# Three token parts for all projection blocks, with the last part beside HGRN in an order written by hand

## The chip, the cores and the metric

The kernel runs on one core of one Trainium2 chip. The metric is the device time of one execution in microseconds (us). The core's engines are named as in the profile: PE (TensorE matmul), PEld (its weight load), DVE (VectorE), ACT (ScalarE), POOL (GpSimd) and SP (SyncE, which here only issues DMAs).

## The reference

One layer of a hybrid mixer over 2048 latent tokens and 256 context tokens of width 1024:

```python
p_lat = (_layer_norm(h_x) * (1.0 + sc_l[:, None]) + sh_l[:, None]) @ w_in[l]
p_ctx = (_layer_norm(h_ctx) * (1.0 + sc_c) + sh_c) @ w_in[l]
pv_l, u_l, fh_l, g_l = _split_proj(p_lat)
...
y_rc, y_rl = _rwkv_branch(u_c, u_l, ...)      # two directions, 6 heads of 64, a state per head
o_hc, o_hl = _hgrn_branch(fh_c, fh_l, ...)    # two directions, 6 heads of 64, chunkwise
pool_l = _pool_branch(pv_l, True, ...)        # centred means over windows of 2, 4, 8, 16
mix_l = jnp.concatenate([pool_l, y_rl, o_hl], axis=-1) * jax.nn.silu(g_l)
new_x = _layer_norm(ALPHA * h_x + gt_l[:, None] * (mix_l @ w_out[l])) * ln_g[l] + ln_b[l]
```

Both scans read the context first and go on over the latent tokens from the context's final state; only the latent output is returned.

## The kernel before

The input projection has 33 blocks of 128 output columns. A projection is made in two fp32r halves: the operands are split into a high part and a rest (`split`: ACT writes the high part, DVE or POOL the difference), and 24 matmuls (high by high, low by high, high by low, over eight slices of the 1024 inputs) sum into one PSUM tile.

The work stands in four stages.

1. *Input stage* (0 to about 500 us): norms, modulation, and the 11 RWKV blocks, group by group of 256 tokens. The modulated input is written to DRAM (`s_x`).
2. *RWKV* (about 500 to 1400): 36 chunks of 64 tokens for both directions. `start` makes the pair products of a chunk (L722, masked on DVE in L724), `gather` and `solve` invert the triangles of four chunks at a time on DVE (L779, L782), `merge` puts the halves together (L831, L841), `late` transposes keys (L744), and `step` carries the state (L858 to L899). The loop runs from n = -7 (`LEAD` chunks ahead) to 35.
3. *HGRN* (about 1400 to 1912): nine windows of 256 tokens for both directions, the first being the context. `hlevels` loads a window, prepares gates and scores and runs six levels; `hsteps` transposes keys, reads out and carries the state chunk by chunk.
4. *Output stage* (1912 to 2152): head norms, gates, the output projection, the last norm.

The other 22 blocks (q, z, i of HGRN, the pooled inputs, the gates) are made beside stages 2 and 3 by the generator `filler(parts, blocks)`. A part is a set of token pieces of up to 512 tokens, 768 in all. For each part `filler` loads the eight slices of the input from `s_x` and splits them into the tiles `fxh` and `fxl`, of which there is one set; then for each block it loads and splits the weights (one block ahead) and projects each piece. It yields after every six matmuls: such a stretch is called a step here, and four steps are a piece. Each piece ends in a sink: to DRAM as it is, to DRAM with tokens on partitions (`to_tokens`, with PE transposes), or through the pooling (`pooled`, scans and differences on DVE).

Before, there were two fillers. The first made 18 blocks (q, z, i, six gates) for three parts beside RWKV, the second made the pooled blocks and the last two gates for three parts of its own beside HGRN. `Beside` runs the steps that have fallen due when RWKV's loop calls it, at four places a chunk; a `BORDER` yield at a part's end makes it pause. In RWKV the order of PE is the order in which the code is written (`manual_schedule`); in HGRN a plan of numbers (`H_LEV`, `H_STP`, `H_FIL`, `H_OW`) gave the order to the scheduler, which placed the instructions of PE, too, by its own estimates. The other engines are ordered by the scheduler throughout. All loads and most stores are issued on SP's queue.

Of the kernel before, what the change touches and what calls it, by code (L numbers as in the profile page):

```python
# [20 lines left out]
P = 128  # L21
D = 1024
KB = 8
# [20 lines left out]
HOLD = 1  # L44

NG_R = 6

# [92 lines left out]
def hybrid_block(ctx: ExitStack, tc: tile.TileContext, x, ctxt, mod_w, w_in, w_up, a_up, pool_w,  # L140
# [388 lines left out]
    def filler(parts, blocks):  # L529

        for part in parts:
            n_all = sum(n for _, n in part)
            xh, xl = [], []
            for k in range(KB):
                xh.append(big.tile([P, FTOK], F32R, name=f"fxh{k}"))
                xl.append(big.tile([P, FTOK], F32R, name=f"fxl{k}"))
                xs = fp.tile([P, FTOK], F32, name="fxs", bufs=2)
                o = 0
                for t0, n in part:
                    QX.dma_start(out=xs[:, o:o + n], in_=s_x[:, k, t0:t0 + n])  # L540
                    o += n
                split(xs[:, 0:n_all], xh[k][:, 0:n_all], xl[k][:, 0:n_all], V)
# [9 lines left out]
            yield BORDER  # L552
# [82 lines left out]
    class Beside:  # L635


        def __init__(self, gen):
            self.gen, self.due, self.hold = gen, 0.0, 0

        def __call__(self, k):
            self.due += k
            if self.hold:
                self.hold -= 1
                return
            while self.due >= 1:
                self.due -= 1
                if next(self.gen, 0) == BORDER:
                    self.hold = HOLD
                    return  # L650
# [17 lines left out]
    with ExitStack() as ph:  # L668
# [239 lines left out]
        def once(f, n):  # L908
# [3 lines left out]
        parts = [[(T, TCTX), (0, 512)], [(512, 512), (1024, 256)], [(1280, 256), (1536, 512)]]  # L912
# [8 lines left out]
        fill1 = filler(parts, blocks)  # L921
        fill = chain(fill1, filler(parts2, blocks2))
# [13 lines left out]
        def beside(n, k):  # L936
            if n >= R_FIL[0]:
                pace(k * R_FIL[1])


        go("sc", 0, start)
        with tc.manual_schedule(engines={mybir.EngineType.PE}):
            for n in range(-LEAD, NCH):
# [33 lines left out]
            run(fill1)  # L977
# [3 lines left out]
    with ExitStack() as ph:  # L981
# [18 lines left out]
        V.tensor_tensor(out=hsl, in0=blk1[:, 0:P:64].unsqueeze(1).broadcast_to([P, 2 * NPR, 2]),  # L1000
                        in1=lb1.unsqueeze(2).broadcast_to([P, 2 * NPR, 2]), op=ALU.mult)
        hdone = [0, 0]

        def hlevels(d, n, w):
# [19 lines left out]
            if lat:  # L1024
                q = fq.tile([P, NPR, HWIN], F32, name=f"q{d}")
                SP.dma_start(out=q, in_=s_q[:, :, tsl].rearrange("b p t -> p b t"))
                qp = wk.tile([P, NPR, HWIN], F32, name=f"qp{d}")
# [23 lines left out]
            if lat:  # L1051
                pd = psl.tile([P, 2, NPR, nm], F32, name="pl")
                for m in range(nm):
                    for p in range(NPR):
                        PE.matmul(pd[:, :, p, m], q[:, p, P * m:P * m + P], hsl[:, 3 * d + p, :], start=True, stop=True)
                V.tensor_tensor(out=sc.rearrange("q h p m t -> q (h p m) t"),
                                in0=cst[:, C_DIAG].unsqueeze(1).broadcast_to([P, 2 * NPR * nm, CH]),
                                in1=pd.rearrange("q h p m -> q (h p m)").unsqueeze(2).broadcast_to(
                                    [P, 2 * NPR * nm, CH]), op=ALU.mult)
# [17 lines left out]
        def hsteps(d, n, w):  # L1077
            lat, tw, t0, ks, it, tot = w["lat"], w["tw"], w["t0"], w["ks"], w["it"], w["tot"]
            kt = stp.tile([P, NPR, nm, P], F32, name=f"kt{d}", bufs=1)
            for p in range(NPR):  # L1080
                pt = pst.tile([P, 512], F32, name="pa")[:, 0:HWIN].rearrange("q (m c) -> q m c", c=P)
                for m in range(tw // P):
# [240 lines left out]
```

## Time and profile before

| | us |
|---|---|
| median of 3 runs (lowest, highest) | 2149.41 (2149.09, 2152.09) |
| profiled execution | 2153.85 |
| its span | 2151.8 |
| PE busy | 1877.4 (87%) |
| DVE busy | 1470.2 (68%) |
| ACT busy | 954.1 (44%) |
| POOL busy | 808.4 (38%) |

Busy times are sums over the whole span and say nothing of the stages apart. PE's clock has two levels, 2.4 and 1.2 GHz; a granted clock of 0.9 is a mean over stretches at 1.0 and at 0.5. Most fp32 matmuls stand in the trace as two records, the fp32r matmuls of the projections as one.

### The profile page before, as it was taken

To read this page: it belongs to the slowest core of one execution; us is meant where nothing else is said; L and a number is where in the kernel's file an instruction comes from. 1 tells how busy PE (TensorE), PEld (TensorE's weight loads), DVE (VectorE), ACT (ScalarE), POOL (GpSimd) and SP (SyncE) were. 2 spreads that over 40 slices of the span, in tenths; PEclk is the share of its full clock that TensorE was granted. 3 is DMA by queue.
4 is the path that set the end of the run, shared out by engine and by line. 5 is a ranking of instruction groups with operands and counts; after the bars stand their busy time and mean duration, and the time that the engine had idled before them with its cause. 6 is when DMAs were issued, how large, how long until landed. Compare 5 with 4: busy or idle time off the path is not lost. (4 is left out here: it accounts for less than half of the span.)

```text
span 2151.8 us, 46723 instructions
## 1 busy us (share of the span) xinstructions
PE 1877.4 (87%) x18306; PEld 1593.8 (74%) x18306; DVE 1470.2 (68%) x3045; ACT 954.1 (44%) x1809; POOL 808.4 (38%) x729
## 2 busy tenths in 40 slices
PE   4788899994989979999979999968989998878996
PEld 1677788893777768877868788757877776657896
DVE  2788899886546646475473762189788788879862
ACT  3876786663123333333333233455444645322321
POOL 0144355545211322322323323454334435624653
PEclk7899999996999989999979999968888997589998
DMA  6544444328655565655666444442322323545531
GB/s 247 195 136 144 142 131 126 106 74 252 187 147 150 171 184 164 182 143 164 174 180 192 139 129 136 152 132 82 109 81 70 124 80 115 176 150 187 194 128 59
DMA packets 290915, 313.68 MB, mean 146 GB/s; under 512 B 85572, under 2 KB 246468, under 8 KB 289672
## 3 DMA queue, kind: packets, MB, share of 16 engines
q1 hardware_dynamic: 280680, 280.29, 43.3%
q10 hardware_dynamic: 4896, 17.83, 2.5%
q0 software_dynamic: 5120, 12.59, 1.8%
q8 instruction: 144, 2.36, 0.5%
q14 instruction: 75, 0.61, 0.1%
HBM read 213.88 MB, written 96.74 MB: 144 GB/s over the span
## 5 line engine op out<-in xcount | busy, mean ns | idle before, releaser
L220 POOL TENSOR_TENSOR fwl<-fwf,fwh 128x1024 fp32r<-128x1024 f32 x66 | 158.7, 2405 | 422.3 <-ACT fwh L219 369.3
L565 PE MATMUL fps<-fxh,fwh 128*128 128x512 f32 (+1 forms) x952 | 230.7, 375 | 31.0 <-ACT fxh L219 28.4
L565 PE MATMUL fps<-fxl,fwh 128*128 128x512 f32 (+1 forms) x952 | 217.2, 362 | 0.0
L565 PE MATMUL fps<-fxh,fwl 128*128 128x512 f32 (+1 forms) x952 | 211.6, 357 | 0.0
L565 PEld LDWEIGHTS fps<-fxh,fwh 128*128 128x128 f32 x952 | 160.4, 201 | 63.4 <-ACT fxh L219 34.7
L565 PEld LDWEIGHTS fps<-fxl,fwh 128*128 128x128 f32 x952 | 160.2, 199 | 24.1 <-issue 1.0
L565 PEld LDWEIGHTS fps<-fxh,fwl 128*128 128x128 f32 x952 | 158.7, 196 | 23.8
L779 DVE TENSOR_TENSOR tm<-m,o 96x31 f32<-96x31 f32 (+15 forms) x279 | 117.4, 421 | 60.3 <-DMA m<-sd 52.2
L904 POOL TENSOR_TENSOR ys<-ys,pp 64x384 f32<-64x384 f32 x64 | 76.6, 1196 | 198.7 <-ACT ys L901 191.6
L336 PE MATMUL ps<-xh,wh 128*128 128x258 f32 x768 | 125.4, 304 | 17.5 <-ACT wh L219 11.9
L1116 DVE SCALAR_TENSOR_TENSOR sbd<-sbd,tot,ps 64x64 f32<-64x64 f32 x432 | 120.5, 279 | 25.7 <-PE ps L1111 16.7
L1044 PE MATMUL pl<-qb,ks 128*64 128x64 f32 x2304 | 108.4, 252 | 30.3 <-DVE sc L1046 22.9
L1039 ACT COPY qb<-qp 64x384 f32<-64x384 f32 x192 | 99.6, 519 | 77.7 <-DVE qp L1069 33.8
L724 DVE TENSOR_TENSOR at<-pa,cst 128x384 f32<-128x384 f32 x144 | 74.1, 548 | 81.9 <-PE pa L722 81.8
L336 PEld LDWEIGHTS ps<-xh,wh 128*128 128x128 f32 x768 | 106.0, 198 | 30.6 <-ACT wh L219 13.3
L1044 PEld LDWEIGHTS pl<-qb,ks 128*64 128x64 f32 x2304 | 94.1, 161 | 45.5 <-issue 29.3
L782 DVE TENSOR_TENSOR o<-o,tm 96x31 f32<-96x31 f32 (+15 forms) x279 | 115.8, 415 | 8.3
L336 PE MATMUL ps<-xh,wl 128*128 128x258 f32 x768 | 118.6, 294 | 0.0
L1069 POOL TENSOR_TENSOR ks<-ks,tot 128x384 f32<-128x384 f32 x90 | 90.5, 1014 | 74.6 <-PE pl L1044 72.7
L336 PE MATMUL ps<-xl,wh 128*128 128x258 f32 x768 | 116.0, 289 | 0.0
L336 PEld LDWEIGHTS ps<-xh,wl 128*128 128x128 f32 x768 | 104.6, 196 | 5.7 <-issue 5.2
L336 PEld LDWEIGHTS ps<-xl,wh 128*128 128x128 f32 x768 | 102.3, 192 | 4.9 <-issue 4.6
(230 smaller groups left out, 4449.0 us busy)
## 6 DMA issues: line engine op xcount, KB each, us to landing
fwf<-in_w_in_dram SPq DMA_DIRECT2D x66, 512.0 KB, 4.2
xt<-in_x_dram ACTq DMA_DIRECT2D x32, 512.0 KB, 4.9
s_kr<-kr SPq DMA_DIRECT2D x54, 256.0 KB, 2.3
s_bk<-bk SPq DMA_DIRECT2D x54, 256.0 KB, 2.5
bks<-s_bk SPq DMA_DIRECT2D x72, 192.0 KB, 3.2
krs<-s_kr SPq DMA_DIRECT2D x72, 192.0 KB, 3.5
bk<-s_bk SPq DMA_DIRECT2D x72, 192.0 KB, 3.0
kr<-s_kr SPq DMA_DIRECT2D x72, 192.0 KB, 3.1
```

Of the source, the lines that this page charges most:

```text
L220: eng.tensor_tensor(out=wl, in0=wf, in1=wh.bitcast(F32), op=ALU.subtract)
L336: PE.matmul(ps[:, 0:TG + 2], a[:, k, :], b[:, k, :], start=(i == 0), stop=(i == 23))
L565: PE.matmul(ps[:, 0:n], a[:, k, :], b[k][:, o:o + n], start=(i == 0), stop=(i == 23))
L724: V.tensor_tensor(out=at[:, h], in0=pa[h], in1=cst[:, C_MASK[d]].unsqueeze(1).broadcast_to([P, NPR, P]), op=ALU.mult)
L779: V.tensor_tensor(out=tv, in0=m[:, j:j + 1, j + 1:32].broadcast_to([nrow, na, nb]), in1=o[:, 0:na, j:j + 1].broadcast_to([nrow, na, nb]), ...
L782: V.tensor_tensor(out=o[:, 0:na, j + 1:32], in0=o[:, 0:na, j + 1:32], in1=tv, op=ALU.subtract)
L904: G.tensor_tensor(out=ys[vr], in0=ys[vr], in1=pp[d][vr], op=ALU.add)
L1039: S.copy(out=qb[hh, :, :, h, :].rearrange("q p c (i b) -> q (p c) i b", b=b), in_=src[hh].rearrange("q p (c i j b) -> q (p c) i j b", c=nc ...
L1044: PE.matmul(pl[64 * (c % 2):64 * (c % 2) + 64, :, p, c // 2, :], ks[:, p, CH * c:CH * c + CH], qb[:, p, c, :, :], start=True, stop=True)
L1069: eng.tensor_tensor(out=v_, in0=v_, in1=tv[:, :, :, 1 - par:2 - par].broadcast_to([P, NPR, nb, b]), op=ALU.mult)
L1116: V.scalar_tensor_tensor(out=sn[hh, p, hh], in0=so_[hh, p, hh], scalar=tot[hh, p, c:c + 1], in1=ps[hh, p, :], op0=ALU.mult, op1=ALU.add)
```

## The change

There is one filler: all 22 blocks for each of three parts (context with tokens 0 to 511; 1280 to 2047; 512 to 1279). Its steps are spread over RWKV and HGRN. Inputs are loaded two slices ahead, across parts too, and the split comes in four pieces of two slices, each ended by a `BORDER`; the pause after a border is gone. RWKV begins with the first part's splits and 20 steps, and then takes 7.6 steps a chunk where it took 9.4. In HGRN the order of PE is written by hand: a window has 14 slots, each with a state step or key transposes of the last window (k, s), a level of this window (l) and `H_FIL` filler steps; the output weights come in the ninth window's slots. The diagonal scores of a window are made with the weights' and the data's roles exchanged, and key transposes are copied out of PSUM in two pieces in place of three.

```diff
-R_FIL = (-6, 9.4)
-H_LEV = (-0.3508, 0.112, 0.0116)
-H_STP = (-0.224, 0.296, 0.047)
-H_FIL = (-0.255, 10.317)
-H_OW = (6.2029, 10.25)
+R_FIL = (20, 7.6)
+H_FIL = (2.2, 1.9, 1.0)
...
-        for part in parts:
+        xs = [load(parts[0], k) for k in range(2)]
+        for pi, part in enumerate(parts):
...
-                split(xs[:, 0:n_all], xh[k][:, 0:n_all], xl[k][:, 0:n_all], V)
+                split(xs[k % 2][:, 0:n_all], xh[k][:, 0:n_all], xl[k][:, 0:n_all], V)
+                if k + 2 < KB:
+                    xs[k % 2] = load(part, k + 2)
+                elif pi + 1 < len(parts):
+                    xs[k % 2] = load(parts[pi + 1], k % 2)
+                if k % 2:
+                    yield BORDER
...
-        parts = [[(T, TCTX), (0, 512)], [(512, 512), (1024, 256)], [(1280, 256), (1536, 512)]]
+        parts = [[(T, TCTX), (0, 512)], [(1280, 256), (1536, 512)], [(512, 512), (1024, 256)]]
...
-                 [(B_G + b, to_dram(s_g[b], AF.Silu)) for b in range(NG_R)]
-        parts2 = [[(0, 512), (512, 256)], [(768, 256), (1024, 512)], [(1536, 512)]]
-        blocks2 = [(B_POOL + b, pooled(b)) for b in range(2)] + \
-                  [(B_G + b, to_dram(s_g[b], AF.Silu)) for b in range(NG_R, 8)]
+                 [(B_POOL + b, pooled(b)) for b in range(2)] + \
+                 [(B_G + b, to_dram(s_g[b], AF.Silu)) for b in range(8)]
...
+            for _ in range(KB // 2):
+                pace(0)
+                next(fill)
+            run(fill, R_FIL[0])
             for n in range(-LEAD, NCH):
...
-            run(fill1)
...
-        hsl = rc.tile([P, 2 * NPR, 2], F32, name="hsl")
+        hsl = rc.tile([P, 2 * NPR, CH], F32, name="hsl")
...
-                        PE.matmul(pd[:, :, p, m], q[:, p, P * m:P * m + P], hsl[:, 3 * d + p, :], start=True, stop=True)
+                            PE.matmul(pd[h][64 * c:64 * c + 64, p], hsl[hh, 3 * d + p, :], qc[:, :, c, :],
+                                      start=True, stop=True)
...
+        slots = ("k0 l0", "k0 l1", "k1 l0", "k1 l1", "s0 l0", "s0 l1", "s1 l0", "s1 l1", "s0 l0", "s0 l1", "s1 l0",
+                 "s1 l1", "l0", "l1")
+        prep = {6: 1, 11: 1}
...
+        with tc.manual_schedule(engines={mybir.EngineType.PE}):
...
+            for n in range(nw + 1):
+                for si, slot in enumerate(slots):
+                    for what in slot.split():
+                        d = int(what[1])
+                        if what[0] == "l" and n < nw:
+                            run(lev[d, n], 1)
+                        elif what[0] != "l" and n > 0:
+                            run(stp_[d, n - 1], 1)
...
+                    if n < nw - 1:
+                        pace(H_FIL[0] if n == 0 else H_FIL[1] if n < 3 else H_FIL[2])
+                    elif n == nw - 1:
+                        run(fill if si == 0 else ow, None if si == 0 else 1)
```

PE where RWKV begins, before (L385 and L435 are the last of the input stage, L722 is a pair product, "fps" a projection; "fxh" and "fxl" are the split inputs):

```order
L385 MATMUL px<-cst,t 128x128 x2
L435 MATMUL px<-t,cst 128x256 x2
L722 MATMUL pa<-krs_6010,bks_6011 128x128 x6
L722 MATMUL pa<-krs_6015,bks_6016 128x128 x6
L722 MATMUL pa<-krs_6032,bks_6033 128x128 x6
L722 MATMUL pa<-krs_6037,bks_6038 128x128 x6
L565 MATMUL fps<-fxh_6080,fwh 128x512
```

The same place now (lines have moved by a few; the rows between are the rest of five pieces):

```order
L379 MATMUL px<-cst,t 128x128 x2
L429 MATMUL px<-t,cst 128x256 x2
L567 MATMUL fps<-fxh_6028,fwh 128x512
L567 MATMUL fps<-fxh_6035,fwh 128x512
...
L567 MATMUL fps<-fxl_6071,fwh 128x512
L567 MATMUL fps<-fxl_6078,fwh 128x512
L720 MATMUL pa<-krs_6010,bks_6011 128x128 x6
L567 MATMUL fps<-fxh_6028,fwh 128x256
```

The first two pair products stood ahead of all projections; now five pieces stand ahead of them.

PE in the third latent window of HGRN, before ("po" is a read-out, L1101 its product with the state "sbd", L1111 "ps" the state's update, L1044 "pl" a level's scores):

```order
L1044 MATMUL pl<-qb_16646,ks_17907 64x2x32 x12
L1044 MATMUL pl<-qb_16648,ks_17931 64x2x32 x12
L565 MATMUL fps<-fxh_18123,fwh 128x256
L1098 MATMUL po<-it_17380,sc_17395 64x64 x6
L1101 MATMUL po<-sbd_16644,qp_17390 64x128 x3
L1111 MATMUL ps<-it_17380,kt_18026 64x64 x2
L1044 MATMUL pl<-qb_16647,ks_17907 64x2x32 x12
L1044 MATMUL pl<-qb_16649,ks_17931 64x2x32 x12
```

Two slots of a window now (read-out, state product, update, level, then six projection matmuls, four of which are left out):

```order
L1102 MATMUL po<-it_16919,sc_17198 64x64 x6
L1105 MATMUL po<-sbd_16281,qp_17193 64x128 x3
L1115 MATMUL ps<-it_16919,kt_18107 64x64 x6
L1043 MATMUL pl<-qb_16286,ks_17651 64x2x32 x12
L567 MATMUL fps<-fxh_15300,fwl 128x256
L567 MATMUL fps<-fxh_15307,fwl 128x256
...
L1102 MATMUL po<-it_16919,sc_17198 64x64 x6
L1105 MATMUL po<-sbd_16282,qp_17193 64x128 x3
L1115 MATMUL ps<-it_16919,kt_18107 64x64 x6
L1043 MATMUL pl<-qb_16288,ks_17663 64x2x32 x12
```

The levels of the two directions stood back to back, and projections stood wherever the scheduler put them; now a level of one direction, a whole state step and six projection matmuls alternate, and two state steps of one direction follow each other.

## Rows read from the trace of the kernel before

**Rows 1.** Windows by stage: stretch, us, busy (records) by engine, clock, DMA, GB/s.

```profile
500.00:1400.00 900.00, 807.18 (x9010) 683.88 (x9010) 477.86 (x1069) 297.03 (x601) 263.36 (x222) 0.93 0.58 166
1400.00:1912.00 512.00, 449.47 (x5122) 366.25 (x5121) 432.87 (x940) 253.98 (x457) 220.72 (x186) 0.82 0.33 104
...
1400.00:1440.00 40.00, 22.95 (x117) 17.99 (x117) 35.54 (x55) 23.15 (x35) 23.58 (x17) 0.60 0.49 148
```

**Rows 2.** Windows of L565 alone (PE, PEld); the last row is all work.

```profile
500.00:1400.00 900.00, 491.41 (x2378) 385.35 (x2378) 0.93 0.58 166
1400.00:1912.00 512.00, 118.58 (x480) 83.52 (x479) 0.82 0.33 104
...
1215.00:1385.00 170.00, 99.31 (x514) 78.01 (x513) 1.00 0.49 139
...
1215.00:1385.00 170.00, 163.50 (x2014) 139.96 (x2013) 66.34 (x132) 63.19 (x138) 60.88 (x57) 1.00 0.49 139
```

**Rows 3.** Chain that ended last: start us, us, what; first state products of RWKV chunks.

```profile
1320.58 1.34 PE py L858 x12
...
1375.25 1.34 PE py L858 x12
```

**Rows 4.** Waits of PE in RWKV: waiter, releaser, us in total, times, longest.

```profile
PE pa L831 <- DVE at L724: 22.6, 9, 4.6
PE fps L565 <- ACT fxh L219: 16.0, 8, 4.7
```

**Rows 5.** Timeline of PE: first state products of two pairs of chunks.

```profile
751.01 1.60 PE L858 MATMUL py<-zbd,kr 128*128 128x128 f32 x12
791.37 1.50 PE L858 MATMUL py<-zbd,kr 128*128 128x128 f32 x12
...
1177.32 1.50 PE L858 MATMUL py<-zbd,kr 128*128 128x128 f32 x12
1202.99 1.50 PE L858 MATMUL py<-zbd,kr 128*128 128x128 f32 x12
```

**Rows 6.** Timeline where RWKV begins (PE, and the first part's last split on DVE).

```profile
516.80 1.65 PE L722 MATMUL pa<-krs,bks 64*128 64x128 f32 x12 [7.45 <-DMA krs<-s_kr]
...
523.58 0.95 DVE L220 TENSOR_TENSOR fxl<-fxs,fxh 128x768 fp32r<-128x768 f32 x1
...
528.02 3.32 PE L565 MATMUL fps<-fxh,fwh 128*128 128x512 f32 x7
...
618.94 1.50 PE L858 MATMUL py<-zbd,kr 128*128 128x128 f32 x12
```

**Rows 7.** Timeline of PE: the diagonal scores of one direction, two windows apart.

```profile
1544.38 2.72 PE L1055 MATMUL pl<-hsl,q 128*128 128x2 f32 x12
...
1654.88 1.50 PE L1055 MATMUL pl<-hsl,q 128*128 128x2 f32 x12
```

**Rows 8.** Timeline of PE in a window of HGRN.

```profile
1626.54 0.91 PE L1098 MATMUL po<-it,sc 64*64 64x64 f32 x12
...
1628.67 0.96 PE L565 MATMUL fps<-fxl,fwh 128*128 128x512 f32 x3
...
1630.70 1.62 PE L1044 MATMUL pl<-qb,ks 128*64 128x64 f32 x48
...
1634.81 0.92 PE L1044 MATMUL pl<-qb,ks 128*64 128x64 f32 x24 [0.75 <-DVE sc L1046]
1637.31 1.55 PE L1044 MATMUL pl<-qb,ks 128*64 128x64 f32 x24 [1.58 <-DVE sc L1046]
```

**Rows 9.** Costliest groups of DVE in HGRN: line, shapes, count, busy us, mean ns, idle before.

```profile
L1116 DVE SCALAR_TENSOR_TENSOR sbd<-sbd,tot,ps 64x64 f32<-64x64 f32 x431 | 120.2, 279 | 25.7 <-PE ps L1111 16.7 <-PE po L1101 0.2
...
L220 DVE TENSOR_TENSOR fxl<-fxs,fxh 128x768 fp32r<-128x768 f32 (+1 forms) x24 | 29.0, 1219 | 1.3 <-ACT fxh L219 0.7 <-PE fps L565 0.3
L610 DVE TENSOR_TENSOR_SCAN fcs<-cst,fpu 128x80 f32<-128x80 f32 x64 | 24.5, 447 | 5.5 <-ACT fpu L608 5.3
...
L618 DVE TENSOR_TENSOR fe<-fcs 64x512 f32<-64x512 f32 (+1 forms) x20 | 16.8, 840 | 0.2
```

More of the change, by code (lines that the diff above doesn't have):

```diff
@@ L529, in filler, with load @@
     def filler(parts, blocks):
-        for part in parts:
+        def load(part, k):
+            xs = fp.tile([P, FTOK], F32, name="fxs", bufs=2)
+            o = 0
+            for t0, n in part:
+                QX.dma_start(out=xs[:, o:o + n], in_=s_x[:, k, t0:t0 + n])
+                o += n
+            return xs
+        xs = [load(parts[0], k) for k in range(2)]
+        for pi, part in enumerate(parts):
             n_all = sum(n for _, n in part)
@@ L997, in hybrid_block @@
                 G.memset(t_, 0.0)
[L999 to L1001 removed]
+        hsl = rc.tile([P, 2 * NPR, CH], F32, name="hsl")
+        V.tensor_copy(out=hsl, in_=lb1.unsqueeze(2).broadcast_to([P, 2 * NPR, CH]))
         hdone = [0, 0]
@@ L1079, in hsteps @@
             kt = stp.tile([P, NPR, nm, P], F32, name=f"kt{d}", bufs=1)
[L1080 to L1085 removed]
+            for ps_ in ((0, 1), (2,)):
+                pt = pst.tile([P, 512], F32, name="pa").rearrange("q (p m c) -> q p m c", p=2, c=P)
+                for i, p in enumerate(ps_):
+                    for m in range(tw // P):
+                        PE.transpose(out=pt[:, i, m, :], in_=ks[:, p, P * m:P * m + P], identity=ident)
+                S.copy(out=kt[:, ps_[0]:ps_[-1] + 1, 0:tw // P, :], in_=pt[:, 0:len(ps_), 0:tw // P, :])
+                yield 1
             ncw = tw // CH
@@ L1137, in hybrid_block, with window @@
         wo = {}
-        plan = []
-        for n in range(1 + T // HWIN):
-            for d in range(2):
-                w = {}
-                lev = hlevels(d, n, w)
-                at(plan, n + H_LEV[0] + H_LEV[2] * d, H_LEV[1], 9, lev)
-                at(plan, n + 1 + H_STP[0] + H_STP[2] * d, H_STP[1], 6, chain(lev, hsteps(d, n, w)))
-        at(plan, H_FIL[0], 1 / H_FIL[1], 300, fill)
-        at(plan, H_OW[0], 1 / H_OW[1], 9, chain(fill, out_weights()))
-        follow(plan)
+        nw = 1 + T // HWIN
+        ow = out_weights()
+        pace = Beside(fill)
+        lev, stp_ = {}, {}
+        slots = ("k0 l0", "k0 l1", "k1 l0", "k1 l1", "s0 l0", "s0 l1", "s1 l0", "s1 l1", "s0 l0", "s0 l1", "s1 l0",
+                 "s1 l1", "l0", "l1")
+        prep = {6: 1, 11: 1}
+        def window(d, n):
+            w = {}
+            lev[d, n], stp_[d, n] = hlevels(d, n, w), hsteps(d, n, w)
+        with tc.manual_schedule(engines={mybir.EngineType.PE}):
+            for d in range(2):
+                window(d, 0)
+                run(lev[d, 0], 2)
+            for n in range(nw + 1):
[6 more added lines that the diff above has]
+                            run(stp_[d, n - 1], 1)
+                    if si in prep and n + 1 < nw:
+                        for d in range(2):
+                            if si == 6:
+                                window(d, n + 1)
+                            run(lev[d, n + 1], 1)
+                    if n < nw - 1:
+                        pace(H_FIL[0] if n == 0 else H_FIL[1] if n < 3 else H_FIL[2])
+                    elif n == nw - 1:
+                        run(fill if si == 0 else ow, None if si == 0 else 1)
+                for d in range(2):
+                    if n < nw:
+                        run(lev[d, n])
+                    if n > 0:
+                        run(stp_[d, n - 1])
+            run(ow)
     mid.close()
```

39 lines of the change are left out of this document (13 added, 26 removed).

## The prediction

> **What bounds the kernel now.** I read the busy time by stage first, then TensorE's waits, then single iterations. The RWKV stage (500 to 1400 us) has PE busy for 807 of 900 us and DVE for 478; the HGRN stage (1400 to 1912) has PE busy for 449 and DVE for 433 of 512, at a granted clock of 0.82, which means that a good third of it ran at the lower of the two levels [rows 1]. So RWKV is a PE stage, and HGRN is loaded on two engines of which neither is full.
>
> In RWKV the projections ("fps") are the larger half: 491 us of PE, 2378 matmuls; HGRN has 480 more [rows 2]. In the undisturbed stretch from 1215 to 1385 at full clock, 514 of them took 99.3 us, 0.193 us each, and PE was busy for 163.5 of 170 us [rows 2]: nothing but PE sets the pace there, 54.7 us for three chunks, 18.2 each [rows 3]. What breaks this pace is of two kinds. In about one chunk in four the block solver fills DVE and PE waits for the masked products (22.6 us in 9 waits) [rows 4]; such a chunk takes 25.7 us [rows 5]. And where a token part ends, PE waits for the split inputs of the next (16 us in 8 waits) [rows 4]; a chunk with that in it took 40.4 us [rows 5]. The lead-in is 102 us from the first pair product to the first state step, and the first projection matmul comes only 11 us into it [rows 6].
>
> HGRN starts badly: from 1400 to 1440 PE is busy for 23 of 40 us at a clock of 0.60 [rows 1], while the second filler splits its first token part. Two of its windows take 110.5 us, 55 each [rows 7].
>
> **The change, part by part.** One filler step is six matmuls, so 6 x 0.193 = 1.16 us [rows 2]; a piece (24 matmuls) is four steps, 4.6 us over both widths.
>
> *Volume.* Before: 18 blocks x 5 latent pieces + 9 context pieces = 99 in RWKV, 4 x 5 = 20 in HGRN. After: 22 x 5 + 9 = 119 again. The total stays; what changes is the place. 20 steps before the loop plus 43 chunks (7 of them lead-in) x 7.6 = 347 steps, less some for borders: about 85 pieces in RWKV and 34 in HGRN. So 14 pieces, five of 512 and nine of 256 tokens, move to HGRN: 14 x 4.6 = 65 us of PE, a little less since the narrow ones prevail.
>
> *RWKV loop.* 36 chunks lose about 2 steps each (9.6 to 7.6): 2.1 to 2.3 us of PE where PE is the pace. I take 27 chunks at 2.1 and the 9 solver chunks, where DVE is late and not PE, at 1: **-66 us**. The ends are -82 (all of it) and 0 (the chain of a chunk shows instead).
>
> *Part borders.* Now the split comes two tiles at a time with two loads running ahead, and PE has RWKV work between; the loads still go through two buffers and the part's tiles are still single, so they wait for the last matmul of the old part. Two borders cost (40.4 - 18.2) + about 20 us before; I take half: **-20 us** (0 to -35).
>
> *Start.* Twenty steps (four pieces of 512 tokens, one of 256) go ahead of the first pair product: 20 x 1.16 = 23 us, a little more since the wide ones prevail. The first can be through no earlier than the splits, the last of which ended at 524.5, and projections began at 528 as it is [rows 6]. So PE fills no idle time here; the lead-in starts later by about the five pieces, and a little is won back by the warm clock: **+22 us** to the first step (0 to +35). It is paid back by the steps that the loop no longer holds, counted above.
>
> *HGRN.* DVE loses three of six input splits, 24 of them, 29.0 us, and six of ten pooled pieces go to RWKV, of whose two largest operations that is 0.6 x (24.5 + 16.8) = 25 us [rows 9]; in RWKV DVE has the room (478 of 900) [rows 1]. HGRN's DVE falls from 433 to about 380 us. PE gains the moved pieces. Per slot of the new fixed order PE has one state step, 1628.67 - 1626.54 = 2.13 us, one level, half of 1.62, 0.81 us [rows 8], and a filler step, 1.16: 4.1 us; eight such slots and six lighter ones (transposes, diagonals, levels alone) make about 46 us a window. DVE has 380 us over the context window and eight others, about 43 a window. I take 52 us, between these and the 55 of before. So: the context window, in which PE has only 31 filler steps, 42 us; the next 52; the third, with 1.9 steps a slot, 46 + 13 x 1.16 = 61, say 63; four at 52; one without filler 48; the one with the output weights 60; the last steps 20. That is 493 us, plus 11 us for the last RWKV chunk's body, 504 against the 537 from 1375 [rows 3] to 1912 before: **-33 us**. The ends: 440 (PE's own sum by the same slots, about 410, and little else), and 493 + 131 (a rival below).
>
> *Edits costed at nothing.* The diagonal scores: 12 records took 1.50 us at full clock [rows 7]. Now there are 24, of 64 columns by 128. If they overlap in pairs as the level matmuls do (48 in 1.62 us for 64 moving columns [rows 8]) they take 1.6 us, otherwise twice that; 16 x 1.6 = 26 us is the other end, and I take 0, the shape being that of the level matmuls. On DVE one masked product a window and direction becomes two of half the size, also 0. Key transposes: three copies become two. Loads: half of the input reloads go; SP's queue is shorter by 40 issues. Five more weight splits fall into HGRN, on POOL and ACT, which are busy for less than half of it (221 and 254 us) [rows 1]; without that cover they would be on the path of the filler alone. The third part's q, z and i must be in DRAM before the fourth window is prepared; in the order its last token transposes stand in the second slot of the third window, five slots (20 us) ahead. If that slips, SP waits at those loads, and the window's other loads and the next weights stand behind them.
>
> **Sum.** -66 - 20 + 22 - 33 = -97 us. The profiled execution took 2153.85 us (span 2151.8), the median of the runs is 2149.41, 4.4 us lower; I take the difference to be the same: **2052 us**. Differences within 0.2% (4.3 us) are about what a measurement of this kernel can't tell from none.
>
> **Rivals.**
> (a) *The forecast*, within some 35 us: 0.56.
> (b) *The RWKV chunk is a chain.* With fewer steps between, the copies out of PSUM and the state update show, and a chunk keeps its 18.2 us. For it: every chunk passes PE, ACT, PE, ACT, PE, DVE. Against it: in the clean stretch PE is idle for 6.5 us in nine chunks only [rows 2], and no wait of a chain is long. Then the 66 us are not won: 2118 us. 0.15.
> (c) *The fixed order stalls in HGRN, slower than before.* One direction's chunk steps stand in neighbouring slots: the six state updates on DVE (6 x 0.279 = 1.7 us [rows 9]) must be through before the next slot's second product. PE does about 2.7 us of other work between, so they fit only if DVE's queue is short, and levels of the other direction are in the same queue. PE waiting for DVE's level operation is in the trace already: 0.75 and 1.58 us [rows 8]. At their mean, 1.17 us, over the 112 slots of eight windows, it costs 131 us: 2183 us. It decides from 97 / 112 = 0.87 us a slot. Against it: the step before a slot's level on PE is ready first on DVE too. 0.11.
> The Trainium skill bears on this ("TensorE: Matmul & The Clock Gate", Part 3, "The mechanism"): matmuls start and end in program order, and only weight loads are pulled ahead. By that rule a waiting product holds up the filler step behind it, which speaks against a rigid order; the waits above agree, since filler stood behind them. It would give the time of (c).
> (d) *Both stages near their floors*: HGRN at 440 us and the loop's whole 82 us, borders at -30: 53 + 16 + 10 more, 1973 us. 0.18.
>
> **How the numbers follow.** (a) is the likeliest: 2052 us. The range takes in (a), (b) and the nearer half of (d): 1990 to 2125; (c), the other half of (d) and little else are left out, 0.2. Slower is (c), 0.11; within 0.2% only if (c) comes out at its tipping point, 0.02; faster is the rest, 0.87.
>
> **What the changed profile would show.** Right: the first step of RWKV near 641 us, chunks of about 16 us in clean stretches, no chunk over 32 us at a border, the last chunk near 1311, no stretch of 40 us at a clock of 0.60 where HGRN starts, windows of 50 to 54 us at a clock above 0.9, HGRN ending near 1815, and the 240 us behind it as before. Wrong: PE idle between projections in clean chunks, released by ACT copies (b); PE in HGRN waiting for DVE state updates or levels in most slots, with the clock near 0.8 (c); diagonals that take twice the time.

## The result, and the profile after

The changed kernel takes 2168.22 us (median of 6 runs, 2160.97 to 2169.73), the kernel before in the same session 2150.75 (6 runs, 2147.78 to 2158.47). The ratio is 1.0069, with a 95% interval of 1.0046 to 1.0092: slower by 0.7%, where 2052 us was forecast. The profiled execution took 2169.2 us, 15.4 more than that of before.

The stages by windows (stretch, length, busy time with records on PE, weight loads, DVE, ACT and POOL, granted clock, DMA share, GB/s), against [rows 1]:

```profile
500.00:1400.00 900.00, 765.69 (x8641) 638.63 (x8642) 509.03 (x1135) 279.70 (x573) 253.25 (x222) 0.91 0.56 158
1400.00:1925.00 525.00, 479.45 (x5683) 397.71 (x5681) 374.06 (x864) 248.65 (x441) 225.35 (x188) 0.87 0.32 101
1925.00:2167.00 242.00, 201.51 (x1252) 181.38 (x1248) 166.20 (x216) 66.11 (x94) 120.41 (x51) 0.91 0.46 156
```

The work went where the change sends it: PE has 41 us less in the RWKV stage and 30 more in HGRN, DVE 31 more and 59 less. The time did not follow. The first and the last state step of RWKV, from the timeline of PE, against [rows 6] and [rows 3]:

```profile
652.07 1.16 PE L856 MATMUL py<-zbd,kr 128*128 128x128 f32 x9
...
1388.67 1.50 PE L856 MATMUL py<-zbd,kr 128*128 128x128 f32 x12
```

So the first step is 33 us later than before (forecast: 22), the last chunk 14 later (forecast: 64 earlier). The loop from the first step to the last chunk takes 737 us, where it took 756: 20 us were won and not 86. From the last chunk's start to the end of HGRN it is 536 us against 537 (forecast: 504), and 242 behind it against 240. 33 - 20 - 1 + 2 gives 14 of the 15.4.

Four chunks in a row of the loop, by windows that begin at each chunk's first state product:

```profile
1148.60:1164.80 16.20, 16.18 (x229) 14.08 (x229) 6.58 (x13) 6.27 (x14) 6.71 (x7) 1.00 0.70 187
1164.80:1184.00 19.20, 17.83 (x237) 15.34 (x237) 8.28 (x14) 6.40 (x14) 5.78 (x5) 1.00 0.67 194
1184.00:1208.40 24.40, 19.06 (x230) 16.15 (x229) 20.82 (x48) 6.40 (x14) 5.38 (x5) 0.86 0.47 130
1208.40:1229.60 21.20, 19.29 (x237) 16.50 (x236) 16.92 (x40) 6.40 (x14) 6.30 (x5) 0.92 0.57 161
```

The first is what was forecast: 16.2 us, PE without a gap, full clock. In the last two, which hold the block solver, DVE is busy for 38 of 46 us, PE has gaps, and the granted clock is 0.86 and 0.92. PE's waits in the loop, against [rows 4]:

```profile
PE pa L829 <- DVE at L722: 31.4, 12, 5.4
PE pa L720 <- DVE at L722: 10.0, 11, 2.4
PE pa L626 <- DVE at L722: 9.4, 3, 4.3
...
PE pa L597 <- DVE at L722: 7.8, 3, 4.2
...
PE fps L567 <- ACT fxh L213: 5.6, 2, 4.0
```

Four waiters for the masked products on DVE (L722), 59 us together, against 30 in the loop of the kernel before. The wait for split inputs was 16.0 us in the whole stage before, 11.9 of them in the loop. Now it is 5.6 in the loop, but 16.5 more stand ahead of it, in the head. The solver's two operations on DVE in the loop (count, busy us, mean ns, idle before), 213 us in 8 groups, 26.6 each:

```profile
L780 DVE TENSOR_TENSOR o<-o,tm 96x31 f32<-96x31 f32 (+15 forms) x248 | 116.0, 468 | 7.2
L777 DVE TENSOR_TENSOR tm<-m,o 96x31 f32<-96x31 f32 (+15 forms) x248 | 97.1, 392 | 34.3 <-DMA m<-sd 27.6
```

How far this bounds the loop is seen in the chain of waits. First a row of the kernel before, not shown ahead, for 1140 to 1300 us, then the changed kernel, 1151 to 1304:

```profile
by line: PE fps L565 44.5%; PE py L858 6.1%; PE py L864 4.9%; PE pu L874 4.8%; PE pa L722 4.4%; DVE o L782 4.0%; PE pa L744 4.0%; PE pu L883 3.7%; PE pu L899 3.2%; DMA nn<-so 3.0%; DVE tm L779 2.9%; PE pa L831 2.8%; issue 2.4%; PE pa L841 2
```

```profile
by line: PE fps L567 23.5%; DVE o L780 15.3%; DVE tm L777 9.8%; DMA m<-sd 4.6%; DVE zbd L887 4.5%; issue 4.3%; DVE tz L885 3.8%; PE pu L872 3.8%; PE py L856 3.5%; PE pa L720 3.4%; PE pa L742 3.4%; DMA nn<-so 3.3%; PE py L862 2.9%; PE pu L88
```

The solver's part of the chain has gone from 7 to 25%, that of the projections from 45 to 24%; over the whole loop of the changed kernel they are 20 and 23%.

HGRN from its third window on (the windows begin at the key transposes):

```profile
1500.80:1570.30 69.50, 65.88 (x766) 54.24 (x765) 56.45 (x134) 34.16 (x60) 28.79 (x25) 1.00 0.31 92
1570.30:1619.30 49.00, 47.75 (x675) 39.68 (x673) 37.27 (x91) 27.40 (x48) 20.48 (x20) 1.00 0.33 101
1619.30:1680.50 61.20, 58.37 (x674) 47.88 (x672) 37.26 (x97) 31.58 (x53) 22.55 (x21) 0.83 0.26 83
...
1779.70:1846.30 66.60, 55.73 (x589) 46.59 (x588) 49.49 (x113) 31.10 (x58) 33.29 (x25) 0.53 0.37 111
1846.30:1900.80 54.50, 49.90 (x591) 42.37 (x590) 33.69 (x76) 12.83 (x26) 20.86 (x19) 0.61 0.35 122
1900.80:1925.10 24.30, 19.80 (x251) 14.27 (x249) 11.92 (x43) 3.52 (x8) 2.19 (x4) 1.00 0.07 26
```

The window at 1570 has 84 projection matmuls and takes 49 us; the one at 1780 has none, fewer instructions on PE, and takes 66.6, at a clock of 0.53.

### The profile page after: what moved, and what is told of

Its sections match the earlier page's. It is cut to its first block, busy times and chain, and to the rows that moved or that the text cites. A ratio compares the mean times of both kernels' runs of the same rounds, so it can differ in the third digit from the quotient of the medians.

```text
span 2167.3 us, 46917 instructions
## 1 busy us (share of the span) xinstructions
PE 1866.9 (86%) x18498; PEld 1581.6 (73%) x18498; DVE 1439.7 (66%) x3037; ACT 930.9 (43%) x1763; POOL 797.8 (37%) x729
## 4 chain that ended last, share of the span: by engine, by line
PE 33%; DVE 23%; DMA 9%; issue 4%; ACT 3%; POOL 3%; SPq 1%; POOLq 0%; DVEq 0%; ACTq 0%
PE fps L567 14%; DVE o L780 5%; DVE tm L777 4%; PE po L1278 2%; PE pl L1043 2%; DVE sbd L1120 2%; PE po L1105 1%; DMA m<-sd 1%; DVE tot L1075 1%; PE po L1102 1%; DVE at L722 1%; PE py L856 1%; DMA nn<-so 1%; PE pa L720 1%; DVE ml L1222 1%
## 5 line engine op out<-in xcount | busy, mean ns | idle before, releaser
L567 PE MATMUL fps<-fxh,fwh 128*128 128x256 f32 (+1 forms) x952 | 228.6, 374 | 29.8 <-ACT fxh L213 22.1
L567 PE MATMUL fps<-fxl,fwh 128*128 128x256 f32 (+1 forms) x952 | 222.1, 365 | 0.0
L567 PE MATMUL fps<-fxh,fwl 128*128 128x256 f32 (+1 forms) x952 | 214.5, 360 | 0.4 <-POOL fwl L214 0.4
L780 DVE TENSOR_TENSOR o<-o,tm 96x31 f32<-96x31 f32 (+15 forms) x279 | 130.6, 468 | 8.1
L777 DVE TENSOR_TENSOR tm<-m,o 96x31 f32<-96x31 f32 (+15 forms) x279 | 109.6, 393 | 36.6 <-DMA m<-sd 29.0
L722 DVE TENSOR_TENSOR at<-pa,cst 128x384 f32<-128x384 f32 x144 | 74.1, 548 | 78.3 <-PE pa L720 78.0
L1043 PE MATMUL pl<-qb,ks 128*64 128x64 f32 x2304 | 102.4, 248 | 13.4 <-POOL ks L1072 9.9
L821 DVE STREAM_TRANSPOSE nn<-nn 32x192 f32<-32x192 f32 x36 | 13.2, 367 | 146.6 <-DMA nn<-so 138.1
L1043 PEld LDWEIGHTS pl<-qb,ks 128*64 128x64 f32 x2304 | 88.6, 158 | 24.7 <-POOL ks L1072 10.5
```

What stands on the lines that cost most here:

```text
L567: PE.matmul(ps[:, 0:n], a[:, k, :], b[k][:, o:o + n], start=(i == 0), stop=(i == 23))
L722: V.tensor_tensor(out=at[:, h], in0=pa[h], in1=cst[:, C_MASK[d]].unsqueeze(1).broadcast_to([P, NPR, P]), op=ALU.mult)
L777: V.tensor_tensor(out=tv, in0=m[:, j:j + 1, j + 1:32].broadcast_to([nrow, na, nb]), in1=o[:, 0:na, j:j + 1].broadcast_to([nrow, na, nb]), ...
L780: V.tensor_tensor(out=o[:, 0:na, j + 1:32], in0=o[:, 0:na, j + 1:32], in1=tv, op=ALU.subtract)
L1043: PE.matmul(pl[64 * (c % 2):64 * (c % 2) + 64, :, p, c // 2, :], ks[:, p, CH * c:CH * c + CH], qb[:, p, c, :, :], start=True, stop=True)
```

## The experiments

All edits are to the changed kernel unless the kernel before is named. Loop means from the first state step to the start of the last chunk. Kernels that leave RWKV's order on PE and DVE as it is came out at 727 to 737 us, so a difference under 10 us in one loop tells nothing; times of the whole are compared through the kernel before on the same chip.

| run | first step | loop, us | against its parent |
|---|---|---|---|
| before / changed | 619 / 652 | 756 / 737 | |
| fewer matmuls, changed / before | 644 / 617 | 696 / 700 | -41 / -57 |
| half the solver, changed / before | 638 / 606 | 697 / 740 | -39 / -16 |
| both, changed | 626 | 653 | -84 |
| masks off DVE | 664 | 747 | +10 |
| DVE's order by hand, sevens / fives | 650 / 654 | 794 / 754 | +58 / +17 |
| no head / more steps in RWKV | 623 / 632 | 738 / 754 | +2 / +17 |

**Is PE the pace? Fewer matmuls.**

```diff
-                                PE.matmul(ps[:, 0:n], a[:, k, :], b[k][:, o:o + n], start=(i == 0), stop=(i == 23))
+                                if i % 4 != 2 or not side["thin"]:
+                                    PE.matmul(ps[:, 0:n], a[:, k, :], b[k][:, o:o + n], start=(i == 0), stop=(i == 23))
```

> The changed kernel, with 6 of the 24 matmuls of every projection piece left out during RWKV (its projections are then not the reference's); the steps and all other work stay. A filler step falls from 1.16 to 0.87 us, so 7.6 steps by 0.29 = 2.2 us of PE per chunk. Theory A (PE sets the pace of RWKV, as the forecast had it): the loop of 737 us from the first to the last state step falls by 27 x 2.2 + 9 x 1 = 68 us, to about 670. Theory B (the solver on DVE holds up the masked products for which PE waits, and what clean chunks win is given back there): clean chunks go from 16.3 to about 14 us, solver chunks grow or stay, and the loop stays above 715.

> The kernel before with the same 6 of 24 matmuls left out during RWKV (projections not the reference's). 9.6 steps by 0.29 = 2.8 us of PE per chunk. Theory A (PE sets the pace there, the step on which the forecast rested): the loop of 756 us falls by 27 x 2.8 + 9 x 1.3 = 87 us, to about 670. Theory B: clean chunks fall to about 15.5, but solver chunks give back what is won, and the loop stays above 725.

The changed kernel's loop fell by 41 us of the 79 that 36 x 2.2 us would be, that of before by 57 of 101. Clean chunks paid in full (16.3 to 14.7 us, 18.4 to 16.4), those with the solver little: in the changed kernel 16 of 23.0 us on average became 18 of 22.1. Neither theory fits: a microsecond off each chunk's projections is worth 0.52 to 0.56 us, in the kernel before as well.

**Is DVE's solver the pace? Half of it.**

```diff
-            for j in range(31):
+            for j in range(0, 31, 2):
...
+                yield 1
+                yield 1
```

> The changed kernel with every second elimination step of the block solver left out (the result is not the reference's); the other steps are handed out over the same time as before. DVE loses about 13 us of work in each group of four chunks, 9 groups. Theory A: PE sets the pace except in the solver chunk itself, so at most some 3 us a group: loop 737 to about 710. Theory B: the chunks of 25 to 30 us fall to 18 to 20 and their neighbours from about 21 to 18, PE's waits for the masks fall from 50 to under 20 us, and the loop goes to 660 to 685.

> The kernel before with every second elimination step of the solver left out (result not the reference's). If its solver chunks were bound by DVE too, the loop of 756 us falls by 30 to 45 us, as the changed kernel's did (39). If PE set its pace, as the forecast read its trace, by at most 9 x 1.5 = 13 us.

> The changed kernel with both lightenings: 6 of 24 projection matmuls left out in RWKV and every second elimination step of the solver left out (neither result is the reference's). Alone they took 41 and 39 us off the loop of 737 us. If PE and DVE bound it in turn, chunk by chunk (clean chunks PE, solver chunks DVE): the sum, about 657 us (645 to 670). If each hides the other everywhere: 620 to 640. If a third thing holds the loop (loads, the chain): 680 to 700.

The changed kernel gained 39 us, between A's 27 and B's 52 or more. The rest of the solver was not handed out over the same time as before: the 32 operations left in a group stand in one chunk for the most part, so the chunks with ten or more are 10 in place of 16. The kernel before gained 16: there the solver was mostly hidden behind the longer PE work, which is what the chain shows as well. Both lightenings together gave 84, almost exactly 41 + 39. So PE and DVE bound the loop in turn: PE in the chunks without solver, DVE's queue in those with it.

**Is it the masks, or the queue?** ACT and POOL take the masked products off DVE.

```diff
-                    V.tensor_tensor(out=at[:, h], in0=pa[h],
-                                    in1=cst[:, C_MASK[d]].unsqueeze(1).broadcast_to([P, NPR, P]), op=ALU.mult)
+                    S.copy(out=at[:, h], in_=pa[h])
+                    G.tensor_tensor(out=at[:, h], in0=at[:, h],
+                                    in1=cst[:, C_MASK[d]].unsqueeze(1).broadcast_to([P, NPR, P]), op=ALU.mult)
```

> The changed kernel with the masked pair products taken off DVE: ACT copies them out of PSUM and POOL multiplies by the mask. The solver on DVE stays as it is. Theory A: no change of the loop by more than 10 us. Theory B: PE's waits for DVE at the masks (31 + 10 + 9 us) go, with them the low clock in the solver chunks, and the loop falls from 737 to 660 to 690; the whole to about 2100. Theory C (a chain from the gathered blocks through DRAM to the solver and back to the merge, over a fixed lead, sets the time of four chunks): the waits move to the merge, and the loop stays above 715.

2186.17 us, ratio 1.013 (1.0079 to 1.0181), the loop 747. PE's waits in the loop:

```profile
PE py L857 <- DVE zbd L888: 35.6, 10, 7.4
PE pa L626 <- DVE fe L623: 17.6, 5, 8.2
```

The waits for the masks are gone, and PE waits about as long for the state update and the pooled differences, which stand in the same queue. So PE does not depend on the masks alone, and theory B's form, the masks, falls. The run does not show what a shorter queue would give, since the queue got no shorter: DVE is busy for 445 us in the loop against 443. The masks' 63.5 us are gone from it, but with them on POOL the solver took 250 us in place of 213, and the state's scaling and the pooled operations 18 more.

**Three edits that did not reach the engines.** Loads of the merge earlier, loads of the solver earlier too, and the solver in fives:

```diff
                 ws[n][d]["uv"] = uv
+            yield 1
...
                 go("late", n + 1, late)
+                go("mer", n + 1, merge)
...
+                if (n + LEAD + 1) % SB == 0:
+                    go("sol", (n + LEAD + 1) // SB - 1, solve)
```

```diff
-                solving(7)
+                solving(5)
...
-                        if SB * g + SB - LEAD <= n < SB * g + SB - LEAD + 2:
+                        if SB * g + SB - LEAD <= n < SB * g + SB - LEAD + 3:
```

> The changed kernel with the loads of the merge (inverted blocks and values) issued at the head of the chunk, half a chunk ahead of the transposes that read them; nothing else moves. In the changed kernel DVE stood still for 138 us in 28 waits for these loads during the RWKV loop (84 us in 22 in the kernel before), and everything behind in DVE's queue stood with it. Theory B2 (DVE's queue in order, which runs late in the solver chunks because of the solver's work and of these waits, sets the pace of four chunks): the waits fall under 40 us, the solver chunks from 25-30 to 20-23, and the loop from 737 to 670 to 700. Theory B (the solver's 26 us of work alone): loop 725 to 740. Theory C (the chain through DRAM over a fixed lead): 690 to 720, the waits staying.

> As the run with the merge's loads early, and the solver's load issued at the end of the chunk before its first step (27.6 us of DVE's waits in 8 in the changed kernel). Theory B2: 5 to 20 us less than the merge's loads early alone. Theory B: no difference between the two. A loss would mean that SyncE, waiting for the gathered blocks to land, holds up the other loads behind it.

> The changed kernel with the block solver handed out in fives instead of sevens, six times a chunk, over up to three chunks: its 62 operations on DVE (26.6 us of a group, 213 us in 8 groups) are spread over 2.1 chunks instead of 1.5; nothing is left out. The rest of DVE's work is 230 us in 36 chunks, 6.4 each. Theory B3 (while the solver runs, DVE's queue is the pace: 26.6 + 1.5 x 6.4 = 36 us in 1.5 chunks, 24 a chunk): now 26.6 / 2.1 + 6.4 = 19 us a chunk, four chunks take 2.1 x 19 + 1.9 x 16.9 = 72 us instead of 82, the loop falls from 737 to about 650 (640 to 690), and the whole by some 85 us. Theory C (the chain through DRAM over a fixed lead): the inverted blocks are ready later, PE waits for the merge, and the loop stays or grows (730 to 780). Theory A: no change over 15 us.

> The kernel before with the same spreading of the solver (fives, up to three chunks), nothing else. If DVE's queue in the solver chunks set the pace there already (B3), four chunks take 2.1 x 19.1 + 1.9 x 18.6 = 75 us instead of 84, and the loop of 756 us falls to 670 to 710. If before PE set the pace (A, as the forecast read its trace), it stays within 15 us. If the chain (C): it grows.

Ratios 1.004 (1.0011 to 1.0069), 1.0089 (1.0062 to 1.0116), 0.9994 (0.9962 to 1.0026) and 0.9987 (0.9954 to 1.0019); loops 727, 736, 735 and, of before, 755. They test nothing: in this program only PE's order is as written, that of DVE and SyncE is made by the scheduler. In the run with the merge's loads early, SyncE's queue still has them behind the gathered blocks, as in the changed kernel:

```profile
1017.42 0.80 SPq L762 DMA_DIRECT2D sd<-tr  x2
1018.31 0.39 SPq L795 DMA_DIRECT2D nn<-so  x1
1018.79 0.39 SPq L733 DMA_DIRECT2D bk<-s_bk  x1
1019.24 0.91 SPq L800 DMA_DIRECT2D nn<-so  x2
```

With the solver in fives, the second and third chunk still hold 34 and 28 of its operations, as with sevens. What DVE's waits for these loads cost (138 us in 28 waits, 84 in 22 before) stays open. That the run in fives took 0.7% less than the changed kernel is no gain of the loop: 15 us of it lie in HGRN, whose code is the same, where the fifth window took 55.4 us at a clock of 0.94 instead of 61.2 at 0.83. In the eleven other traces whose HGRN is that of the changed kernel it took 521 to 542 us from the last chunk on, and 562 in one of them; a difference inside that range tells nothing.

**The solver spread in earnest.** DVE's order in RWKV fixed as written, with sevens and with fives:

```diff
-        with tc.manual_schedule(engines={mybir.EngineType.PE}):
+        with tc.manual_schedule(engines={mybir.EngineType.PE, mybir.EngineType.DVE}):
```

> The changed kernel with DVE's order in RWKV fixed as written, the solver in sevens as it was written before: the control for the fives. By B3 the loop is 720 to 760, as in the changed kernel (737), and 30 us or more above that with fives. If fixing the order by itself is what helps, the two come out alike.

> The changed kernel with DVE's order in RWKV fixed as written, like PE's, and the solver written in fives over up to three chunks (the run with fives alone had left DVE's rows as they were). Theory B3 (DVE's queue in the solver chunks sets the pace): 26.6 / 2.1 + 6.4 = 19 us in a solver chunk, four chunks 72 us instead of 82, the loop 737 to 650-700. Theory C (the chain through DRAM over a fixed lead): the inverted blocks come later and PE waits for the merge, 730 to 780. If the loop stays at 720 to 740 with the solver spread, it is neither, and half clock or waits of other kinds are to be read from the trace.

2216.95 us (one run) with sevens, 2192.93 (ratio 1.0149, 1.0101 to 1.0198) with fives. The profiled execution with fives took 2210.15 us, the longest of its four; its HGRN, whose code is the same, took 562 us against 529 with sevens, so only the loops are compared: 794 and 754. Four chunks with sevens, then with fives:

```profile
1236.50:1260.60 24.10, 18.08 (x231) 15.60 (x229) 21.10 (x48) 6.40 (x14) 5.43 (x5) 0.86 0.45 128
1260.60:1286.90 26.30, 19.92 (x236) 17.12 (x235) 18.67 (x41) 6.39 (x14) 5.38 (x5) 0.87 0.53 139
1286.90:1308.60 21.70, 19.32 (x237) 16.69 (x236) 7.64 (x13) 6.39 (x14) 5.79 (x5) 0.92 0.38 107
1308.60:1325.00 16.40, 16.31 (x230) 14.04 (x229) 6.73 (x13) 6.40 (x14) 5.60 (x5) 1.00 0.36 92
```

```profile
1212.00:1232.60 20.60, 17.86 (x231) 15.42 (x230) 17.54 (x42) 6.40 (x14) 5.79 (x5) 0.92 0.52 150
1232.60:1252.20 19.60, 17.78 (x237) 15.23 (x236) 18.04 (x43) 6.29 (x14) 5.94 (x5) 1.00 0.54 154
1252.20:1273.80 21.60, 19.21 (x237) 16.64 (x236) 8.43 (x17) 6.40 (x14) 5.79 (x5) 0.92 0.53 137
1273.80:1290.30 16.50, 16.42 (x231) 14.13 (x230) 6.73 (x13) 6.40 (x14) 5.60 (x5) 1.00 0.32 86
```

The same work on both engines, 88.5 us against 78.3: with at most 18 us of DVE in a chunk PE's gaps are smaller, and the clock is 0.92 and 1.00 in the first two chunks instead of 0.86 and 0.87. That agrees with B3's mechanism, with one profile on either side. The expected 650 to 700 us were missed: a fixed order on DVE costs 58 us by itself, and the loop with fives stays 17 us above the changed kernel's.

**The pooled blocks.** Their work on DVE left out in RWKV (scans and differences, in `pooled`).

```diff
+            if side["ps"] is psa:
+                pd_ = pool.tile([P, 512], F32, name="fe", bufs=2)
+                S.copy(out=pd_[:, 0:n], in_=ps)
...
+                return
```

> The changed kernel with the scans and differences of the pooled blocks left out where these fall into RWKV (their result is then not the reference's); the projection matmuls and the copies stay. The forecast costed them at nothing in RWKV, since DVE has the room: loop 735 to 740. Theory B2: about 25 us of DVE's work, much of it in solver chunks; the two chunks of 28 to 30 us with pooled work in them fall to 24 to 26, the loop by 10 to 25 us.

The loop is 730 us, 7 less: within the scatter, and at most the lower end of what B2 expected. Costing them at nothing was not the error.

**The end of HGRN.** The projections spread over one window more:

```diff
-H_FIL = (2.2, 1.9, 1.0)
+H_FIL = (2.2, 1.9, 0.75)
```

> The changed kernel with 0.75 in place of 1.0 projection steps a slot from the fourth window of HGRN on, so that the same projections last one window longer. In the changed kernel the first window without projections ran at a granted clock of 0.53 and took 66 us, where windows with them took 49 to 50. If the clock explains that window, it takes 50 to 55 us and the others stay at 50: the whole 10 to 16 us shorter. If it was not the clock but a chain of the window's own, it stays at 62 to 66, and the whole gets no shorter.

2155.95 us, ratio 0.9992 (0.9960 to 1.0024), 0.8% below the changed kernel's ratio, as far below as the solver in fives came (0.9994), which left HGRN alone. The windows that answer to those from 1779.70 on:

```profile
1773.80:1821.20 47.40, 44.58 (x651) 37.35 (x648) 36.57 (x94) 26.68 (x48) 20.39 (x19) 0.96 0.30 93
1821.20:1876.70 55.50, 50.33 (x601) 43.16 (x599) 43.35 (x88) 18.65 (x37) 26.84 (x21) 0.64 0.24 73
1876.70:1912.70 36.00, 31.77 (x252) 24.35 (x250) 15.89 (x49) 6.00 (x12) 13.98 (x8) 0.50 0.63 214
```

The first has 60 projection matmuls more and takes 47.4 us instead of 66.6, at 0.96 instead of 0.53. By the expectation the clock, not a chain, made that window long. The other traces do not bear this out. Twelve, the changed kernel's among them, hold this window without projections, and it took 64.0 to 67.8 us in all of them, whatever its clock (0.53 to 0.69) and PE's busy time (55.7 to 47.4 us). The one with the highest clock, from the run with the merge's and the solver's loads early:

```profile
1775.40:1839.40 64.00, 47.36 (x588) 38.94 (x588) 51.70 (x112) 29.84 (x55) 32.01 (x23) 0.69 0.30 94
```

The edit moved something else as well: the splits of the output weights, half of which write to the tiles that the projections read. In the changed kernel 14 of their 16 operations on DVE stand in this window, with the late filler one. In the changed kernel's window:

```profile
L214 DVE TENSOR_TENSOR fxl<-fwf,fxh 128x768 fp32r<-128x768 f32 x7 | 8.5, 1219 | 9.1 <-ACT fxh L213 9.1
L214 DVE TENSOR_TENSOR wol<-fwf,woh 128x256 fp32r<-128x256 f32 x7 | 4.1, 588 | 0.0
```

The ninth window, which has no projections and at most two of the splits in those twelve traces, does follow its clock: 41.7 us at 0.89 (solver in fives), 54.5 at 0.61 (changed kernel). That points to the output weights for the eighth, but no run takes them out of it and leaves it without projections, so whether they, the clock or both make it long stays open. A gain of the whole is not shown either: 12 of these 19 us are given back in the last steps, which now run at half clock (36.0 us against 24.3), and HGRN's 524 us from the last chunk on lie within the 521 to 542 of the traces without this edit.

**The head, and how many steps RWKV takes.**

```diff
-R_FIL = (20, 7.6)
+R_FIL = (0, 8.06)
```

```diff
-R_FIL = (20, 7.6)
+R_FIL = (0, 8.9)
...
-H_FIL = (2.2, 1.9, 1.0)
+H_FIL = (0.9, 0.9, 0.9)
```

> The changed kernel with no projection steps ahead of the first pair product, and 8.06 instead of 7.6 steps a chunk, so that about the same number of steps falls into RWKV. The forecast charged the head with 22 us, the trace showed the first state step at 652 instead of 619. If the head costs its PE time there, the first step comes back to 619 to 627 and the loop grows by 0.46 x 1.16 = 0.5 us a chunk at most (19 us): the whole 10 to 25 us less. If the splits of the first part are what is late, the first step stays above 640.

> As without the head, but with 8.9 instead of 8.06 projection steps a chunk in RWKV and 0.9 a slot throughout HGRN, so that about 35 steps move from HGRN into RWKV. If PE sets the pace of the loop (A): 0.84 x 1.16 = 1 us a chunk, 738 to 773 us. If DVE's solver chunks do (B3): at most the clean chunks grow, 738 to 750. In HGRN 35 steps by 1.16 = 40 us of PE leave the first three windows, of which the third took 70 us at full clock: HGRN falls by 15 to 40 us, or stays if its clock falls with them.

Without the head: 2127.52 us (one run; the kernel before 2153.99 beside it). The first step is at 623 and the loop at 738: the 20 steps cost 29 us ahead of the loop, and the 16 of them that moved into it cost nothing there that a scatter of 10 us would show. HGRN, at 525 us, is 11 shorter, which is within its scatter. With 8.9 steps a chunk the whole took 2140.95: the loop grew by 15 of the 35 us that these steps are, HGRN from the last chunk on fell from 525 to 515.

**Together.**

> The changed kernel with the spread solver and the late filler of HGRN together. If the two act in stages that do not touch each other, the gains add: some 85 us by B3 and 15 us measured for the late filler, about 2070 us. By C no faster than the late filler alone (2155).

> The changed kernel without the projection head before RWKV (8.06 steps a chunk) and with 0.75 steps a slot from the fourth window of HGRN on. Alone the first took 41 us off the profiled run and the second 13; they act 700 us apart. If they add: 2110 to 2120 us, 2% below the kernel before. If the late filler's gain is only a clock that differs from run to run, it stays at 2127 to 2140.

The solver in fives with the late filler took 2157.12 us (ratio 0.9999, 0.9966 to 1.0033): as the late filler alone, and as the fives alone, which reach no engine. No head and the late filler: 2128.63 us, ratio 0.9881 (0.9848 to 0.9915). That beats both kernels, 1.2% below the one before and 1.9% below the changed one, with two numbers of the change altered. But without the head alone it was 2127.52 already, so the late filler adds nothing here. That is the other outcome in the expectation, 2127 to 2140, for a gain that is only a clock that differs from run to run; what is left is the head.

## Why the prediction was wrong

- **Step price and clean chunks: right.** 16.2 to 16.9 us where a chunk is undisturbed, as "about 16" said. Rival (b), a chunk that is a chain, falls: where nothing else is in the way the microseconds come.
- **The RWKV loop, -66: the step that failed.** It took three undisturbed chunks [rows 2, 3] for 27 of 36. They stand at the loop's end, behind the solver's last operation (1294 us). In truth 16 of 35 chunks hold ten solver operations or more, before as now, and a group of four chunks holds 26.6 us of them. They were packed into 1.5 chunks, with 6.4 us of other DVE work each: 24 us a chunk. That is above the 18.2 us of the old clean chunk, but there halving the solver gave only 16 us; above 16.3 it stands bare (39 us). Halving, thinning and both (-39, -41, -84) show it, and the spread at a fixed order (-40) agrees. By the measured 0.55 us per us, 36 chunks by 2.1 us are worth 42, not 66. Of these, apart from the two border chunks, only 6 came (677 to 671 us): 19 clean chunks of 19.4 us became 17 of 17.8, which won some 27 us, and 14 solver chunks of 22.1 became 16 of 23.0, which gave 20 back. So where the step put a gain of 1 us on 9 solver chunks, 14 lost 0.9 each, and there are two more of them. Some 7 us of that loss may be the pooled blocks; the rest, with scatter of 10, was not settled; the longer waits of DVE for the merge's loads are one candidate that no run reached. The clock explains little: its mean over the loop is 0.94, against 0.95 before.
- **Borders, -20: half right.** The two chunks went from 40.4 and 38.5 to 30.5 and 35.0, -13, and PE's wait for splits in the loop shrank from 11.9 to 5.6. But before, 71 solver operations ran inside these two stalls; now 9 do, and the others stand in ordinary chunks.
- **Start, +22: mis-sized.** 33, of which the head is 29 (no head: 623). The steps, most of them over 512 tokens, cost 1.45 us each on average and not 1.16. "Paid back by the steps that the loop no longer holds" was wrong for the same reason as the loop.
- **HGRN, -33: right in its windows, wrong at its end.** Windows with a step a slot took 49 to 50 us (forecast 52) but for one of 61, which took 54 to 55 at a clock of 0.94 to 0.97 in five other traces; the third 69.5 (63). The window without projections was put at 48 us and took 66.6. The step left its clock where it was and counted the output weights in the ninth window; the trace shows a clock of 0.53 and 14 of 16 splits of these weights here, 12.6 us of DVE. Which of the two it was stays open. Of the 32 us missed that is 19, the third window 7. DVE's 374 us are what the step said (380).
- **Costed at nothing.** The diagonals took 22.3 us for 384 records, as the 16 x 1.5 of before: right. Nothing waited for the third part's q, z and i: the fourth window is one of 49 us.
- **Rivals.** (c), the end on the slower side, did not happen by its mechanism: PE's waits for the state update in HGRN come to 8.6 us, not 131. It became slower through none of the four; the two that mattered, DVE's queue as the next bound in RWKV and the slow window without projections, were not among them.

The Trainium skill ("TensorE: Matmul & The Clock Gate", Part 1, "What's actually happening") says that the low clock is the default state and that activity releases it. The traces agree as far as they go: this window was granted 0.53 to 0.69 without projections, and 0.96 to 1.00 in the four traces with 60 to 72 projection matmuls in it. These differ in the output weights' splits as well.

## What to carry to other kernels

A clean stretch shows the pace of clean iterations only; before taking work off the bounding engine, add up the next engine's queue over the whole period of the pattern (here four chunks), where its burst stands, since that is the new floor. Before a low clock is called the cause of a slow stretch, look at that stretch in every trace that holds it: here it took 64 to 68 us at clocks from 0.53 to 0.69. And after an edit of the order, look whether the engine meant has got it: here a scheduler undid four.

## What the hardware showed unexpectedly

The window of HGRN without projections had PE busy for 55.7 of 66.6 us, and was granted a clock of 0.53 all the same; in eleven other traces it was granted 0.53 to 0.69, for 64.0 to 67.8 us.

An operation of the solver takes 0.33 us on average, but 1.18 where it overlaps a tensor operation of POOL (64 of 558 in the changed kernel, up to 2.97 us): some 54 us of DVE in all. On DVE and on POOL, from the timeline:

```profile
1027.17 0.42 DVE L780 TENSOR_TENSOR o<-o,tm 96x256 f32<-96x256 f32 x1
...
1028.90 2.24 DVE L780 TENSOR_TENSOR o<-o,tm 96x255 f32<-96x255 f32 x1
...
1028.51 2.35 POOL L214 TENSOR_TENSOR fwl<-fwf,fwh 128x1024 fp32r<-128x1024 f32 x1 [9.32 <-ACT fwh L213]
```

The Trainium skill ("SBUF — State Buffer", "SBUF: two separate sides") describes a port pair that DVE and POOL share, and that one of them holds for a whole instruction; these rows agree. With the masks on POOL, 94 of the 496 operations in the loop overlapped in place of 58. No run took POOL's work away, so what it costs the loop was not measured.
